# SwiGLU computed token-major with its norm gain in the activations, one token tile ahead at the mixer boundary, conformer taps in their own buffers

## The chip, the cores and the metric

One core of one Trainium2 chip runs the whole program. The metric is the device time of one execution in microseconds (us). Three executions of the kernel before are on record, and their median counts. Five engines work from queues of their own: TensorE (PE: matmuls and transposes), VectorE (DVE), ScalarE (ACT), GpSimd (POOL), and SyncE (SP), which issues nearly all transfers here.

## What is computed

One layer of a mixer and feed-forward block on 256 tokens, width 2048, feed-forward width 5632, all in float32:

```python
h = rms_norm(x, mix_pre_g)
proj = h @ w_in                       # hyena input, conformer a and b, two gates
hy_in, cf_a, cf_b = proj[..., :s1], proj[..., s1:s2], proj[..., s2:s3]
gate_a, gate_b = proj[..., s3:s4], proj[..., s4:]
...                                   # y_a: hyena long convolutions of hy_in
u = cf_a * sigmoid(cf_b)
u = depthwise_conv(u, cf_dw_w, cf_dw_b)          # the taps
y_b = silu(layer_norm(u, cf_ln_g, cf_ln_b))
merged = sigmoid(gate_a) * (y_a @ hy_proj) + sigmoid(gate_b) * (y_b @ cf_proj)
x = x + rms_norm(merged @ w_out, mix_post_g)
h = rms_norm(x, ffn_pre_g)
gu = h @ ffn_w_gu
gate, up = gu[..., :FFN_HIDDEN], gu[..., FFN_HIDDEN:]
x = x + rms_norm((silu(gate) * up) @ ffn_w_down, ffn_post_g)
```

## The kernel before

**Split products.** Each large matrix product is made of three rounded ones. An operand is split into a rounded part `hi` and the rest `lo`, and hi by hi, lo by hi and hi by lo are added up in PSUM. The activations are split once. The weights come as groups of 512 KB (2 x 128 rows by 512 columns): SP loads a group into one of four `raw` buffers (L288), ACT rounds it to `hi` (L301), DVE subtracts to get `lo` (L302); `hi` and `lo` have three buffers each, or come as `spare` ones from a pool of 35 slots called `big`. PE's matmuls are recorded on one line, L87.

**Stages.** In order: the input products with the hyena filters and convolutions; the gate chunks (weight `w_as`, 8 chunks of 512 columns each), beside which conformer and layer norm run; the two projections `hy_proj` and `cf_proj`; `w_out`; SwiGLU (`w_gu`, 11 gate chunks and 11 up chunks of 512 columns in turn); `w_down`. PSUM has four buffers called `main` and four called `aux`.

**Two forms of a chunk.** `chunk_as` is token-major: the split activations of 128 tokens are the stationary operand and 512 columns of weight move, so a chunk takes 96 matmuls 512 wide (8 groups, 2 halves, 2 token tiles, 3 products), in two PSUM buffers. `chunk_hl`, which SwiGLU uses, is feature-major: 128 columns of weight are stationary, and both token tiles and both parts of the activations move at once, 512 wide, for hi; for lo, 256 tokens move. That is 64 matmuls 512 wide and 64 matmuls 256 wide, in four buffers. There the norm's gain is multiplied into the weight in the split (ACT L306, DVE L307, two instructions each for a group), and 1/rms of each token is laid out along the free dimension by `per_token` (two matmuls at L450) and multiplied in twice on DVE (L1119, L1121).

**Order.** Each engine takes its instructions in the order of its queue. A scheduler of the framework sets that order from the program's order, priorities and dependences; `keep_in_program_order` and `in_order` (with the names L201 and L217 in the trace) pin some of it. The small steps of hyena, conformer, layer norm and norms are Python generators. `pump(budget)` runs a few of their steps after each weight group, so where their instructions stand depends on how many yields they make.

**The places the change touches.** `conformer` (L830) takes a `raw` buffer and a `hi` buffer of the weight rings for its taps: five small loads by SP (L835, L837), a cast on ACT (L839), a subtraction on DVE (L840). `layer_norm` transposes its result on PE (16 transposes, L890) and then, for four pairs of 128 features, runs two sigmoids on ACT (L897), two scalings on DVE (L898), a product on DVE (L900), a cast on ACT (L904) and a subtraction on DVE (L905). A gate chunk's PSUM buffers are emptied by ACT with a sigmoid (L811). At the mixer boundary, `turn` transposes the new residual stream for SwiGLU (PE L1012) and splits it (ACT and DVE, L201). `turn(0, ...)` handles token tile 0 while `w_out` ends. `turn_second` handles token tile 1, two feature tiles at a time, between the matmuls of SwiGLU's first chunk; it is preceded by `residual` (DVE L1003), and `keep_warm` puts 10 and 5 matmuls there whose result nobody reads.

Of the kernel before, what the change touches and what calls it, by code (L numbers as in the profile page):

```python
# [53 lines left out]
def block_kernel(ctx: ExitStack, tc: tile.TileContext, a: dict, out: bass.AP):  # L54
# [226 lines left out]
    def split_group(src, spare=False, gain=None, on=direct):  # L281

# [7 lines left out]
        return split_raw(raw, spare, gain, on)  # L290

    def split_raw(raw, spare=False, gain=None, on=direct, parts=False):
# [6 lines left out]
        if gain is None:  # L299
            for k in range(2) if parts else (slice(0, 2),):  # L300
                S.copy(hi[:, k], raw[:, k])  # L301
                V.tensor_tensor(out=lo[:, k], in0=raw[:, k], in1=hi[:, k], op=ALU.subtract)  # L302
        else:
# [87 lines left out]
    def product_as(w, nkt, act, budget, late, done):  # L391


        ps = [[aux() for _ in range(4)], [
            psm.tile([P, 512], F32, tag="main", name=nm("main")) for _ in range(4)]]
        groups = [(kt, hf) for kt in range(nkt) for hf in range(2)]
# [10 lines left out]
        held = []  # L407
        for i, (kt, hf) in enumerate(groups):
            ahead = i >= len(groups) - late
# [420 lines left out]
    def conformer(hf):  # L830
        cs = slice(hf * 512, (hf + 1) * 512)
        raw = wp.tile([P, 2, 512], F32, tag="raw", name=nm("raw"), bufs=4)
# [5 lines left out]
        wt = wp.tile([P, 2, 512], F32R, tag="hi", name=nm("hi"))  # L838
# [114 lines left out]
    drain(list(evac))  # L953
    evac.clear()
# [51 lines left out]
    def turn(t, kps):  # L1006

        ps = aux().rearrange("p (k q t) -> p k q t", k=2, t=P)
# [253 lines left out]
```

## Time and profile before

| what | value |
|---|---|
| three executions | 1409.57 to 1412.51 us, median 1412.0 |
| profiled execution | 1413.79 us, of it 1412.0 us in the profile's span |
| PE busy | 1392.8 us (99%) |
| DVE busy | 950.2 us (67%) |
| ACT busy | 740.2 us (52%) |
| SwiGLU, 715 to 1162 us | 20 chunks of 22.35 us each |

The profile follows the chain of work that ended last back from the last instruction. Where PE fills that chain, the time is the sum of PE's instructions plus the gaps between them; another engine's work counts only where PE waits for it. In the timeline, an instruction's own duration runs longer than the distance between two starts, since matmuls overlap: sums here use the distance between starts. A figure in square brackets behind a row is idle time of that engine just before it, with what ended it.

### The profile page before, as it was taken

How to read it: one execution, taken by the hardware profiler on the slowest of the kernel's cores; microseconds unless marked ns; L12 is line 12 of the kernel's file. 1: busy time of each engine (PE TensorE's matmuls, PEld its weight loads, DVE VectorE, ACT ScalarE, POOL GpSimd, SP SyncE). 2: the span in 40 equal slices, each digit the busy share in tenths (PEclk: the TensorE clock that was granted, in tenths of full speed). 3: DMA queues.
4: the chain of work that ended last, by engine and by line, in shares of the span. 5: the costliest groups of instructions: out<-in, count | busy, mean ns of one | idle time of the engine just before them, and what ended most of it. 6: DMA issues, size and time to landing. Idle time of an engine off the chain costs nothing.

```text
span 1412.0 us, 18734 instructions
## 1 busy us (share of the span) xinstructions
PE 1392.8 (99%) x7070; PEld 1183.2 (84%) x7070; DVE 950.2 (67%) x1378; ACT 740.2 (52%) x1093; POOL 11.0 (1%) x23
## 2 busy tenths in 40 slices
PE   9999999999899999999999999999999999999997
PEld 8788888888778888887888888888888888888885
DVE  5997978888878466547776767666666765444445
ACT  6665655455555444345665555555565654333343
POOL 0010000000000000000000000000000000000000
PEclk9999999999999999999999999999999999999999
DMA  9776554454455665765556666666666666666553
GB/s 331 216 211 179 171 188 147 148 152 133 153 173 167 196 189 179 273 197 171 163 186 190 181 195 189 193 184 191 189 185 193 185 190 222 194 193 193 193 188 128
DMA packets 76554, 264.70 MB, mean 187 GB/s; under 512 B 8689, under 2 KB 10002, under 8 KB 76464
## 3 DMA queue, kind: packets, MB, share of 16 engines
q1 hardware_dynamic: 75520, 261.74, 59.9%
q0 software_dynamic: 944, 1.77, 0.4%
q8 instruction: 55, 0.90, 0.2%
q14 instruction: 35, 0.29, 0.1%
HBM read 261.38 MB, written 2.10 MB: 187 GB/s over the span
## 4 chain that ended last, share of the span: by engine, by line
PE 93%; DMA 3%; DVE 2%; ACT 1%; issue 0%; DVEq 0%; SPq 0%; ACTq 0%
PE main L87 61%; PE aux L87 31%; DMA raw<-in_w_down_dram 1%; DMA raw<-in_w_out_dram 1%; DVE lo L302 1%; ACT big L301 0%; DVE big L302 0%; DMA raw<-in_w_gu_dram 0%; PE aux L1012 0%; DMA big<-in_xT_dram 0%; PE aux L934 0%; PE aux L620 0%; PE aux L704 0%; ACT hi L301 0%; PE aux L577 0%
## 5 line engine op out<-in xcount | busy, mean ns | idle before, releaser
L302 DVE TENSOR_TENSOR lo<-raw,hi 128x1024 fp32r<-128x1024 f32 x276 | 336.7, 1222 | 222.9 <-ACT hi L301 203.8
L301 ACT CAST hi<-raw 128x1024 fp32r<-128x1024 f32 x276 | 290.5, 1054 | 372.4 <-PE main L87 312.2
L87 PE MATMUL main<-hi,big 128*128 128x512 f32 x1440 | 369.8, 390 | 1.7 <-ACT hi L301 1.7
L307 DVE SCALAR_TENSOR_TENSOR lo<-raw,pv,hi 128x512 fp32r<-128x512 f32 x342 | 243.0, 747 | 153.0 <-ACT hi L306 150.6
L306 ACT ACTIVATE hi<-raw,pv 128x512 fp32r<-128x512 f32 x342 | 228.5, 716 | 188.3 <-PE aux L87 86.6
L87 PEld LDWEIGHTS main<-hi,big 128*128 128x128 f32 x1440 | 269.4, 188 | 57.9 <-ACT hi L301 2.2
L87 PE MATMUL main<-big,hi 128*128 128x512 f32 (+1 forms) x1152 | 278.9, 384 | 2.6 <-DVE t L734 1.2
L87 PEld LDWEIGHTS main<-big,hi 128*128 128x128 f32 x1152 | 201.5, 192 | 37.2 <-ACT hi L217 2.2
L87 PE MATMUL main<-lo,big 128*128 128x512 f32 x720 | 203.5, 390 | 2.0 <-DVE lo L302 2.0
L87 PE MATMUL aux<-big,hi 128*128 128x512 f32 x704 | 176.5, 392 | 0.0
L87 PEld LDWEIGHTS main<-lo,big 128*128 128x128 f32 x720 | 134.8, 188 | 30.7 <-DVE lo L302 2.6
L87 PEld LDWEIGHTS main<-big,lo 128*128 128x128 f32 x1088 | 149.1, 191 | 10.7
L87 PE MATMUL main<-big,lo 128*128 128x256 f32 x1088 | 152.9, 283 | 0.0
L87 PEld LDWEIGHTS aux<-big,hi 128*128 128x128 f32 x704 | 126.5, 189 | 22.6
L87 PE MATMUL aux<-hi,big 128*128 128x512 f32 x416 | 112.4, 389 | 0.0
L87 PEld LDWEIGHTS aux<-big,lo 128*128 128x128 f32 x704 | 96.2, 190 | 7.0
L87 PE MATMUL aux<-big,lo 128*128 128x256 f32 x704 | 98.3, 282 | 0.0
L87 PEld LDWEIGHTS aux<-hi,big 128*128 128x128 f32 x416 | 78.0, 188 | 16.2
L87 PE MATMUL aux<-big,big 128*128 128x512 f32 x288 | 78.3, 394 | 1.1 <-ACT big L301 0.8
L87 PE MATMUL aux<-lo,big 128*128 128x512 f32 x208 | 64.8, 389 | 0.0
L87 PEld LDWEIGHTS aux<-big,big 128*128 128x128 f32 x288 | 53.1, 188 | 13.8 <-ACT big L301 2.0
L87 PEld LDWEIGHTS aux<-lo,big 128*128 128x128 f32 x208 | 39.1, 188 | 8.1
(223 smaller groups left out, 804.9 us busy)
## 6 DMA issues: line engine op xcount, KB each, us to landing
raw<-in_w_gu_dram SPq DMA_DIRECT2D x176, 512.0 KB
raw<-in_w_as_dram SPq DMA_DIRECT2D x96, 512.0 KB
raw<-in_w_down_dram SPq DMA_DIRECT2D x88, 512.0 KB
raw<-in_w_in_dram SPq DMA_DIRECT2D x44, 512.0 KB
raw<-in_w_out_dram SPq DMA_DIRECT2D x32, 512.0 KB
raw<-in_hy_proj_dram SPq DMA_DIRECT2D x16, 512.0 KB
raw<-in_cf_proj_dram SPq DMA_DIRECT2D x16, 512.0 KB
raw<-in_w_in_dram SPq DMA_DIRECT2D x8, 256.0 KB
```

Of the source, the lines that this page charges most:

```text
L87: return nc.tensor.matmul(o, lhsT, rhs, start=start, stop=stop, skip_group_check=True)
L301: S.copy(hi[:, k], raw[:, k])
L302: V.tensor_tensor(out=lo[:, k], in0=raw[:, k], in1=hi[:, k], op=ALU.subtract)
L306: S.activation(hi[:, k], raw[:, k], AF.Identity, scale=g)
L307: V.scalar_tensor_tensor(out=lo[:, k], in0=raw[:, k], scalar=g, in1=hi[:, k], op0=ALU.mult, op1=ALU.subtract)
```

## The change

- **Taps.** The conformer's taps and their split get buffers from the slots of `big`, and the generator yields three times between the loads and the cast.
- **SwiGLU token-major.** `chunk_hl`, `joined` and the uses of `per_token` go. SwiGLU's chunks are `chunk_as`. The gain is applied where the activations are split: `turn` makes 128 x 128 instructions, one for each feature tile with its gain, in place of one for two feature tiles. 1/rms is a scale for each partition, in the Silu (L1103) and in the product on DVE (`glu_by`, L816). The product of both is token-major and is turned back for `w_down` by 8 PE transposes for each pair of chunks (L1113), then split (L1115, L1116).
- **First chunk.** `first_gate` runs token tile 0 of groups 0 to 2 ahead of tile 1, puts `turn_second` between, drops `keep_warm`, and splits from group 3 on one group ahead, with the split's instructions pinned behind `turn`'s on ACT and DVE.
- **`product_as`** (`w_out`, `w_down`) takes the first half of the columns for four row tiles before the second half, asks for its PSUM buffers in two steps, and drains waiting evacuations at the second step, where it had been done ahead of the stage.

```diff
-    def split_group(src, spare=False, gain=None, on=direct):
+    def split_group(src, spare=False, on=direct):
...
-            for k in range(2):
-                g = pv[:, gain + k:gain + k + 1]
-                S.activation(hi[:, k], raw[:, k], AF.Identity, scale=g)
-                V.scalar_tensor_tensor(
-                    out=lo[:, k], in0=raw[:, k], scalar=g, in1=hi[:, k],
-                    op0=ALU.mult, op1=ALU.subtract)
...
     def product_as(w, nkt, act, budget, late, done):
-        ps = [[aux() for _ in range(4)], [
-            psm.tile([P, 512], F32, tag="main", name=nm("main")) for _ in range(4)]]
-        groups = [(kt, hf) for kt in range(nkt) for hf in range(2)]
+        ps = [[], []]
+        first = 4
+        groups = [(kt, hf) for hf in range(2) for kt in range(first)]
+        groups += [(kt, hf) for kt in range(first, nkt) for hf in range(2)]
...
     def conformer(hf):
         cs = slice(hf * 512, (hf + 1) * 512)
-        raw = wp.tile([P, 2, 512], F32, tag="raw", name=nm("raw"), bufs=4)
+        raw = slot([P, 2, 512])
...
-        wt = wp.tile([P, 2, 512], F32R, tag="hi", name=nm("hi"))
+        wt = slot([P, 2, 512], F32R)
+        for _ in range(3):
+            yield None
         nc.scalar.copy(wt[:96], raw[:96])
...
     def turn(t, kps):
...
-        for i, kp in enumerate(kps):
-            turned.append(in_order(nc.scalar).copy(h2T[kp][:, :, 0, t * P:(t + 1) * P], ps[:, i]))
-        for i, kp in enumerate(kps):
-            d = h2T[kp][:, :, :, t * P:(t + 1) * P]
-            in_order(nc.vector).tensor_tensor(
-                out=d[:, :, 1, :], in0=ps[:, i], in1=d[:, :, 0, :], op=ALU.subtract)
+        parts = [(i, kp, q, pv[:, G_FFN + 2 * kp + q:G_FFN + 2 * kp + q + 1])
+                 for i, kp in enumerate(kps) for q in range(2)]
+        for i, kp, q, g in parts:
+            turned.append(S.activation(
+                h2T[kp][:, q, 0, tokens], ps[:, i, q], AF.Identity, scale=g))
+        for i, kp, q, g in parts:
+            V.scalar_tensor_tensor(
+                out=h2T[kp][:, q, 1, tokens], in0=ps[:, i, q], scalar=g,
+                in1=h2T[kp][:, q, 0, tokens], op0=ALU.mult, op1=ALU.subtract)
...
-            keep_warm(10, *warm)
         turn(1, (kp,))
         if kp == 0:
-            keep_warm(5, *warm)
             last()
...
-        per_token(rB, rstd2, psm.tile([P, 512], F32, tag="main", name=nm("main")))
...
-    def chunk_hl(w, col, gain, pool, tag, budget, turn=None):
...
+    def first_gate(w, budget):
+        ps = [psm.tile([P, 512], F32, tag="main", name=nm("main")) for _ in range(2)]
         on = (in_order(nc.scalar), in_order(nc.vector))
+        groups = KT // 2
+        parts = [split_group(w[g]) for g in range(3)]
+        def mms(g, t, ks=(0, 1)):
+            hi, lo = parts[g]
+            for k in ks:
+                av = h2T[g][:, k, :, t * P:(t + 1) * P]
+                for s, m in ((0, hi), (1, hi), (0, lo)):
+                    tc.keep_in_program_order(mm(
+                        ps[t], av[:, s], m[:, k, :], (g, k, s) == (0, 0, 0) and m is hi,
+                        (g, k) == (groups - 1, 1) and m is lo))
+        mms(0, 0)
+        mms(1, 0)
+        mms(2, 0, (0,))
+        turn_second(0)
+        mms(2, 0, (1,))
+        turn_second(1)
+        mms(0, 1)
+        for g in range(2, groups):
+            turn_second(g)
+            if g + 1 < groups:
+                parts.append(split_group(w[g + 1], g < 5, on))
+            mms(g - 1, 1)
+            if g + 1 < groups:
+                mms(g + 1, 0)
             pump(budget)
+        mms(groups - 1, 1)
         return ps
...
     def silu(ps, sg):
...
-            nc.vector.tensor_tensor(out=s, in0=s, in1=rB2, op=ALU.mult)
-            nc.scalar.activation(s, s, AF.Silu)
-            nc.vector.tensor_tensor(out=s, in0=s, in1=rB2, op=ALU.mult)
...
+        for t in range(2):
+            nc.scalar.activation(sg[:, t], ps[t], AF.Silu, scale=rstd2[:, t:t + 1])
+        yield 0.1
+    def glu(ps, sg, dst):
+        yield from glu_by(ps, sg, (rstd2[:, 0:1], rstd2[:, 1:2]))
         for i in range(2):
+            tr = aux().rearrange("p (c t) -> p c t", t=T)
+            for c in range(2):
+                for t in range(2):
+                    f = (2 * i + c) * P
+                    nc.tensor.transpose(tr[:, c, t * P:(t + 1) * P], sg[:, t, f:f + P], ident)
             d = dst[i]
-            nc.scalar.copy(d[:, :, 0, :], v)
-            nc.vector.tensor_tensor(out=d[:, :, 1, :], in0=v, in1=d[:, :, 0, :], op=ALU.subtract)
+            nc.scalar.copy(d[:, :, 0, :], tr)
+            nc.vector.tensor_tensor(out=d[:, :, 1, :], in0=tr, in1=d[:, :, 0, :], op=ALU.subtract)
...
-            chunk_hl(a["w_gu"], n * 512, G_FFN, psm, "main", 1.1,
-                     turn_second if n == 0 else None), sg))
+        after_chunk(silu(first_gate(w_gu[0], 1.2) if n == 0 else chunk_as(w_gu[n], h2T, 1.2), sg))
         before_chunk()
-        ps = chunk_hl(a["w_gu"], FFN + n * 512, G_FFN, psa, "aux", 1.1)
+        ps = chunk_as(w_gu[FFN // 512 + n], h2T, 1.2)
```

**Where instructions stand: the second load of the taps.** ACT's queue. `hi<-raw` at L301 (L299 now) is a weight group's cast; the cast of the taps is L839 (L841 now). Before:

```order
L301 CAST hi_3415<-raw_3413 128x1024
L301 CAST hi_3439<-raw_3437 128x1024
L680 COPY t_652_3290<-aux_3276 128x512
L839 CAST hi_3464<-raw_3457 96x1024
L301 CAST hi_3469<-raw_3467 128x1024
L711 ACTIVATE t_662_3337<-aux_3332,il_135 128x128
```

After:

```order
L662 CAST big_3431<-t_717_3551 128x512
L299 CAST hi_3908<-raw_3906 128x1024
L680 COPY t_733_3650<-aux_3635 128x512
L299 CAST hi_3926<-raw_3924 128x1024
L811 ACTIVATE big_3439<-main_3440,rstdx_124 128x512
L811 ACTIVATE big_3439<-main_3441,rstdx_124 128x512
L841 CAST big_3393<-big_3386 96x1024
L299 CAST hi_3965<-raw_3963 128x1024
L299 CAST hi_4004<-raw_4002 128x1024
```

On SP's queue the taps' loads stood directly ahead of the load of `raw_3467`, whose cast follows theirs on ACT. Now ten weight groups (`raw_3701` to `raw_3963`) are loaded between the taps' loads and the taps' cast.

**Layer norm, on ACT.** L897 (L899 now) is its sigmoid, L904 (L906) its cast, L811 the sigmoid that empties a gate chunk's PSUM. Before:

```order
L897 ACTIVATE t_827_4061<-aux_4056,pv 128x256
L301 CAST hi_4237<-raw_4235 128x1024
L897 ACTIVATE t_835_4095<-aux_4090,pv 128x256
L904 CAST big_4069<-t_829_4067 128x2x256
L301 CAST hi_4255<-raw_4253 128x1024
L897 ACTIVATE t_835_4095<-aux_4090,pv 128x256
L301 CAST hi_4273<-raw_4271 128x1024
L897 ACTIVATE t_843_4129<-aux_4124,pv 128x256
L904 CAST big_4103<-t_837_4101 128x2x256
L811 ACTIVATE big_3883<-main_3884,rstdx_124 128x512
L811 ACTIVATE big_3883<-main_3885,rstdx_124 128x512
L301 CAST hi_4294<-raw_4292 128x1024
```

After:

```order
L299 CAST hi_4332<-raw_4330 128x1024
L899 ACTIVATE t_822_4045<-aux_4040,pv 128x256 x2
L899 ACTIVATE t_830_4079<-aux_4074,pv 128x256
L906 CAST big_4053<-t_824_4051 128x2x256
L899 ACTIVATE t_830_4079<-aux_4074,pv 128x256
L899 ACTIVATE t_838_4113<-aux_4108,pv 128x256
L906 CAST big_4087<-t_832_4085 128x2x256
L899 ACTIVATE t_838_4113<-aux_4108,pv 128x256
L899 ACTIVATE t_849_4152<-aux_4147,pv 128x256
L906 CAST big_4121<-t_840_4119 128x2x256
L811 ACTIVATE big_3880<-main_3881,rstdx_124 128x512
L811 ACTIVATE big_3880<-main_3882,rstdx_124 128x512
```

Before, a weight cast stood between each two steps of layer norm, and L811 empties `main_3884` behind three of its four pairs. Now no weight cast stands between; the L811 for `main_3881` has the same place behind three pairs.

**Layer norm, on PE.** The last of its 16 transposes (L890, L892 now) and what follows. Before:

```order
L890 MATMUL aux_4124<-ident,big_3654 128x128
L890 MATMUL aux_4124<-ident,big_3655 128x128
L890 MATMUL aux_4124<-ident,big_3654 128x128
L890 MATMUL aux_4124<-ident,big_3655 128x128
L87 MATMUL main_4139<-hi_4142,big_115 128x512
L87 MATMUL main_4138<-lo_4143,big_115 128x512
L87 MATMUL main_4139<-lo_4143,big_115 128x512
L87 MATMUL main_4138<-lo_4143,big_115 128x512
L87 MATMUL main_4139<-lo_4143,big_115 128x512
L87 MATMUL main_4138<-hi_4165,big_116 128x512 x2
```

After:

```order
L892 MATMUL aux_4147<-ident,big_3652 128x128
L892 MATMUL aux_4147<-ident,big_3653 128x128
L892 MATMUL aux_4147<-ident,big_3652 128x128
L892 MATMUL aux_4147<-ident,big_3653 128x128
L87 MATMUL main_4125<-lo_4274,big_122 128x512
L87 MATMUL main_4126<-lo_4274,big_122 128x512
L87 MATMUL main_4125<-lo_4274,big_122 128x512
L87 MATMUL main_4126<-lo_4274,big_122 128x512
L87 MATMUL main_4290<-hi_4294,big_115 128x512 x4
```

Before, the transposes stood after the first 7 of the 96 matmuls of the chunk in `main_4138` and `main_4139`, so 89 followed. Now they stand ahead of the last 4 matmuls of the chunk in `main_4125` and `main_4126`; then comes the next chunk in `main_4290`, which takes over the buffer of `main_3881`.

**First chunk of SwiGLU, on PE.** L1012 (L1014 now) is a transpose of `turn_second`. Before, one group:

```order
L1012 MATMUL aux_5941<-ident,big_5122 128x128 x2
L87 MATMUL main_5823<-big_5132,hi_5845 128x512
L87 MATMUL main_5824<-big_5132,hi_5845 128x512
L87 MATMUL main_5825<-big_5132,hi_5845 128x512
L87 MATMUL main_5826<-big_5132,hi_5845 128x512
L87 MATMUL main_5823<-big_5132,lo_5846 128x256
L87 MATMUL main_5824<-big_5132,lo_5846 128x256
L87 MATMUL main_5825<-big_5132,lo_5846 128x256
L87 MATMUL main_5826<-big_5132,lo_5846 128x256
```

After, one group:

```order
L1014 MATMUL aux_5953<-ident,big_5105 128x128 x2
L87 MATMUL main_5839<-big_5911,big_5115 128x512 x2
L87 MATMUL main_5839<-big_5912,big_5115 128x512
L87 MATMUL main_5839<-big_5911,big_5115 128x512 x2
L87 MATMUL main_5839<-big_5912,big_5115 128x512
L87 MATMUL main_5838<-big_5963,big_5117 128x512 x2
L87 MATMUL main_5838<-big_5964,big_5117 128x512
L87 MATMUL main_5838<-big_5963,big_5117 128x512 x2
L87 MATMUL main_5838<-big_5964,big_5117 128x512
L1014 MATMUL aux_5979<-ident,big_5105 128x128 x2
```

Between two pairs of transposes there were 8 matmuls 512 wide and 8 matmuls 256 wide of groups split three ahead. Now there are 12 matmuls 512 wide: 6 of tile 1 with the group before (`big_5911`) and 6 of tile 0 with the group just split (`big_5963`).

## Rows read from the trace of the kernel before

**Rows 1.** The page: shares of the chain that ended last, by engine.

```profile
PE 93%; DMA 3%; DVE 2%; ACT 1%; issue 0%; DVEq 0%; SPq 0%; ACTq 0%
```

**Rows 2.** The chain in order of time: start, us, engine and line.

```profile
440.81 71.20 PE main L87 x314
...
1139.88 22.35 PE aux L87 x128
```

**Rows 3.** Busy time by window, PE first: SwiGLU, and the start of w_down.

```profile
715.00:1162.00 447.00, 447.00 (x2563) 393.31 (x2562) 299.39 (x482) 260.06 (x442) 0.00 (x0) 1.00 0.63 189
1162.00:1190.00 28.00, 28.00 (x126) 23.18 (x126) 15.89 (x18) 13.03 (x17) 0.00 (x0) 1.00 0.68 227
```

**Rows 4.** Timeline of PE at the second load of the taps.

```profile
358.28 2.11 PE L87 MATMUL main<-hi,big 128*128 128x512 f32 x8 [1.71 <-ACT hi L301]
...
365.68 1.21 PE L87 MATMUL main<-lo,big 128*128 128x512 f32 x4 [2.04 <-DVE lo L302]
```

**Rows 5.** Timeline of ACT, then of SP, at the second load of the taps.

```profile
356.24 1.05 ACT L839 CAST hi<-raw 96x1024 fp32r<-96x1024 f32 x1 [4.46 <-PE aux L704]
...
345.49 0.95 SPq L835 DMA_DIRECT2D raw<-in_cf_dw_w_dram  x3
```

**Rows 6.** Timeline of PE, matmuls 512 and 256 wide in one chunk.

```profile
696.90 1.12 PE L87 MATMUL aux<-big,lo 128*128 128x256 f32 x8
697.86 2.00 PE L87 MATMUL aux<-big,hi 128*128 128x512 f32 x8
```

**Rows 7.** The chain at the 16 transposes of layer norm.

```profile
439.06 1.75 PE aux L890 x16
```

**Rows 8.** Timeline of ACT in layer norm.

```profile
439.76 0.57 ACT L897 ACTIVATE t<-aux,pv 128x256 f32<-128x256 f32 x1 [2.10 <-PE aux L890]
440.94 0.56 ACT L897 ACTIVATE t<-aux,pv 128x256 f32<-128x256 f32 x1 [0.61 <-DVE t L898]
...
442.84 0.62 ACT L904 CAST big<-t 128x512 fp32r<-128x512 f32 x1
...
453.94 1.27 ACT L811 ACTIVATE big<-main,rstdx 128x512 f32<-128x512 f32 x2
```

**Rows 9.** Timeline of DVE in layer norm.

```profile
441.54 0.54 DVE L898 TENSOR_SCALAR t<-aux,pv 128x256 f32<-128x256 f32 x1 [0.64 <-ACT t L897]
442.12 0.69 DVE L900 TENSOR_TENSOR t<-t,t 128x512 f32<-128x512 f32 x1
442.73 1.22 DVE L302 TENSOR_TENSOR lo<-raw,hi 128x1024 fp32r<-128x1024 f32 x1
```

**Rows 10.** The chain at the mixer boundary and the first chunk.

```profile
664.28 2.28 PE aux L87 x10
...
667.22 1.15 PE aux L87 x5
...
672.43 0.22 PE aux L1012 x2
...
715.01 0.22 PE main L450 x2
```

**Rows 11.** Timeline of DVE, then ACT (two rows), at the boundary and at L711.

```profile
666.22 0.48 DVE L1003 SCALAR_TENSOR_TENSOR big<-big,por,big 128x256 f32<-128x256 f32 x1
...
672.68 0.37 ACT L201 CAST big<-aux 128x256 fp32r<-128x256 f32 x1 [0.74 <-PE aux L1012]
...
358.14 0.36 ACT L711 ACTIVATE t<-aux,il 128x128 f32<-128x128 f32 x1
```

**Rows 12.** Busy time by window of 1 us, granted clock third from the end.

```profile
46.00:47.00 1.00, 0.00 (x0) 0.00 (x0) 1.00 (x4) 0.03 (x1) 0.00 (x0) 1.00 1.12 252
47.00:48.00 1.00, 0.92 (x3) 0.81 (x4) 1.00 (x4) 1.00 (x3) 0.00 (x0) 0.78 0.92 145
...
50.00:51.00 1.00, 1.00 (x4) 0.79 (x3) 1.00 (x4) 0.00 (x0) 0.00 (x0) 0.52 0.91 307
...
350.00:360.00 10.00, 8.29 (x42) 6.67 (x40) 4.72 (x6) 4.35 (x11) 0.00 (x0) 1.00 0.48 139
```

More of the change, by code (lines that the diff above doesn't have):

```diff
@@ L289, in split_group, with split_raw @@
         latest[:] = [raw]
-        return split_raw(raw, spare, gain, on)
-    def split_raw(raw, spare=False, gain=None, on=direct, parts=False):
+        return split_raw(raw, spare, on)
+    def split_raw(raw, spare=False, on=direct, parts=False):
         if spare:
@@ L298, in split_raw @@
         S, V = on
[L299 to L303, printed above, removed]
-            for k in range(2):
-                g = pv[:, gain + k:gain + k + 1]
-                S.activation(hi[:, k], raw[:, k], AF.Identity, scale=g)
-                V.scalar_tensor_tensor(
-                    out=lo[:, k], in0=raw[:, k], scalar=g, in1=hi[:, k],
-                    op0=ALU.mult, op1=ALU.subtract)
+        for k in range(2) if parts else (slice(0, 2),):
+            S.copy(hi[:, k], raw[:, k])
+            V.tensor_tensor(out=lo[:, k], in0=raw[:, k], in1=hi[:, k], op=ALU.subtract)
         return hi, lo
@@ L407, in product_as @@
         held = []
+        before_chunk()
         for i, (kt, hf) in enumerate(groups):
+            if kt == 0:
+                if hf:
+                    drain(list(evac))
+                    evac.clear()
+                ps[0] += [aux() for _ in range(2)]
+                ps[1] += [psm.tile([P, 512], F32, tag="main", name=nm("main")) for _ in range(2)]
             ahead = i >= len(groups) - late
@@ L1049, in block_kernel @@
     post_norm(a["w_out"], KT, mT, "mix_post_g", "po", 1.3, 8, finish_mixer, turn_first)
-    rB = const.tile([P, 1, T], F32, name="rB")
     def h_norm():
@@ L1058, in h_norm @@
             rms_rstd(rstd2[:, t:t + 1], ss2[:, t, :], f"pf{t}")
-        yield None
-        per_token(rB, rstd2, psm.tile([P, 512], F32, tag="main", name=nm("main")))
         done.add("h_norm")
-    rB2 = rB.broadcast_to([P, 2, T])
-    def chunk_hl(w, col, gain, pool, tag, budget, turn=None):
-        ps = [pool.tile([P, 2, T], F32, tag=tag, name=nm(tag)) for _ in range(4)]
-        def split(g):
-            ahead.append(split_group(
-                w[col // 512, g], gain=gain + 2 * g, on=on if turn and g > 2 else direct))
-        ahead = deque()
-        on = (in_order(nc.scalar), in_order(nc.vector))
-        if turn:
-            for g in range(3):
-                split(g)
-            turn(0)
-        for g in range(KT // 2):
-            if not turn:
-                split(g)
-            hi, lo = ahead.popleft()
-            for k in range(2):
-                for c in range(4):
-                    m = mm(ps[c], hi[:, k, c * P:(c + 1) * P], h2T[g][:, k],
-                           g == 0 and k == 0, False)
-                    if turn:
-                        tc.keep_in_program_order(m)
-                if turn and k == 0 and g + 1 < KT // 2:
-                    turn(g + 1)
-            for k in range(2):
-                for c in range(4):
-                    m = mm(ps[c][:, 1, :], lo[:, k, c * P:(c + 1) * P], h2T[g][:, k, 0, :],
-                           False, g == KT // 2 - 1 and k == 1)
-                    if turn:
-                        tc.keep_in_program_order(m)
-            if turn and g + 3 < KT // 2:
-                split(g + 3)
@@ L1124, in glu @@
-    def glu(ps, sg, dst):
-        up = slot([P, 4, T])
-        yield from joined(ps, up)
-        for i in range(2):
-            v = up[:, 2 * i:2 * i + 2, :]
+        for t in range(2):
[3 more added lines that the diff above has]
+        yield from glu_by(ps, sg, (rstd2[:, 0:1], rstd2[:, 1:2]))
+        for i in range(2):
+            tr = aux().rearrange("p (c t) -> p c t", t=T)
[3 more added lines that the diff above has]
+                    nc.tensor.transpose(tr[:, c, t * P:(t + 1) * P], sg[:, t, f:f + P], ident)
@@ L1129, in glu @@
             d = dst[i]
[L1130 to L1133 removed]
+            nc.scalar.copy(d[:, :, 0, :], tr)
+            nc.vector.tensor_tensor(out=d[:, :, 1, :], in0=tr, in1=d[:, :, 0, :], op=ALU.subtract)
+            yield 0.7
+    w_gu = a["w_gu"]
     for n in range(FFN // 512):
```

21 lines of the change are left out of this document (3 added, 18 removed).

## The prediction

> **What bounds the kernel now.** I read the chain's shares first: PE fills 93% of it [rows 1]. The chain in order of time then shows long pieces of PE with nothing between, 314 matmuls in 71.20 us and twenty chunks of SwiGLU at 22.35 us each [rows 2]; by windows PE is busy without a gap over the whole of SwiGLU and the start of `w_down` [rows 3]. So two things change the time: how many us of instructions PE has, and where PE waits. The work that the change takes off DVE and ACT inside SwiGLU (two products with 1/rms, one gain in each split) is worth nothing by itself, since PE never waits for them there. Then I looked at the three places where the change alters what PE waits for: the taps, layer norm, and the first chunk.
>
> **Taps: -3.75.** PE waits 1.71 us for a cast and 2.04 us for the subtraction a little later [rows 4]. The releaser named is a weight's cast, but that cast stood behind the taps' cast (L839), which ACT began at 356.24 after 4.46 us idle; the taps had been issued by SP at 345.49 [rows 5], so they took 10.7 us to be of use. Now ten weight groups lie between their loads and their cast. A group is 12 matmuls in a gate chunk, 71.20 / 314 = 0.2268 us each [rows 2], so 2.72 us; ten, less the four that the `raw` buffers let SP run ahead, are 16 us, more than 10.7. The wait goes: -3.75. If the loads were later still, the sum would lack it.
>
> **Layer norm: +8.4, and +1.7 for the clock.** The three extra yields and the later loads move the conformer about a chunk back, and layer norm with it. Its 16 transposes stood at the start of a gate chunk, with 89 matmuls (20.2 us) behind them for PE; now 4 matmuls stand between them and a chunk whose first PSUM buffer is emptied by an L811 that stands on ACT behind three of layer norm's four pairs. I count from the first transpose, y. PE: 1.75 [rows 7] and 4 x 0.2268, done at y + 2.66. ACT: the weight cast ahead of layer norm needs the buffer that PE frees at y, so it ends about 1.35 later (1.05 for such a cast by L839 [rows 5], 0.3 to its start), and the first sigmoid begins at y + 1.35. DVE's scaling follows 0.60 later (440.94 to 441.54 [rows 8, 9]); then 0.46, a weight's subtraction that now stands between (1.22, 1.14 apart), and 0.58 to the product (441.54 to 442.12 [rows 9]): y + 4.13. The cast of the pair starts 0.72 behind the product (442.12 to 442.84 [rows 8, 9]): y + 4.85. A further pair costs DVE product, scaling, subtraction and scaling at 0.61, 0.69 (waiting for the cast), 0.63 and 0.58, so 2.5 us; two make the third cast start at y + 9.95. It takes 0.50, and the L811 0.63 for one tile (1.27 for two [rows 8]): y + 11.1. PE waits 11.1 - 2.66 = **8.4**. Before, the same L811 began at 453.94 [rows 8], some 7 us ahead of the chunk that needed its buffer (440.8 + 89 x 0.2268 = 461.0), which is why no wait shows. The range: nothing if the emptying came first; 10 if a step of ACT or DVE here takes as long as in the trace of before, where a pair lasted 5 us between weight casts.
>
> After an idle stretch PE starts slower. PE stood idle through 46 to 47 us, and the granted clock was then 0.78 in the next us and 0.52 in the fourth, half in between; the four lose 0.22 + 0.50 + 0.50 + 0.48 = 1.7 us. With 8.3 of 10 us busy the clock stayed at full level [rows 12]. An idle stretch of 8 us is like the first: **+1.7**, with 0 and 3.5 as ends.
>
> **First chunk and boundary: +2.45, and +1.7 for the clock.** Before, from the end of `w_out` at 664.28 to the end of the second chunk at 715.23 are 50.95 us [rows 10]. Of these, `keep_warm` is 3.43 (2.28 + 1.15) and `per_token` 0.44 (two pieces of 0.22) [rows 10]. Now the two chunks are 192 matmuls of 0.2268, 43.55 us, and the 16 transposes cost 1.75 as before [rows 7]: 45.3 without waits, 5.65 less. `keep_warm` was no loss while PE had to wait anyway, so I count the waits that come:
> - Ahead of `turn_second(0)`: 15 matmuls (3.4 us) cover to 667.7. The first `residual` began on DVE at 666.22 [rows 11]; DVE now has 16 instructions of 128 columns in place of 8 of 256 ahead of it (0.25 apart on ACT by L711 [rows 11], a little more on DVE), about 1.5 later. It ends at 668.2 to 668.7: 0.9.
> - Ahead of `turn_second(1)`: 3 matmuls cover 0.7 of the split, `last()` and the next `residual`, 2.2 in all: 1.5.
> - Groups 3 to 6. After two transposes (0.22) ACT splits them, beginning 0.41 after the transposes began (672.43 against about 672.7 [rows 10, 11]), two at 0.25, then the group's cast, 1.05: `hi` is ready at 1.97. DVE's subtraction, 1.22 [rows 9], makes `lo` ready at 3.2. PE has 6 matmuls to fill, to 1.58; it waits 0.4 for `hi`, does two, waits 0.8 for `lo`, does four. A group takes 4.14 instead of 2.94: 4 x 1.2 = 4.8. Before, the weights were split further ahead and PE had no such wait: from 672.43 on only the transposes' 0.22 lies between long pieces.
> - The last group and the start of the second chunk, two casts and two subtractions against 14 matmuls: 0.9.
>
> Together 8.1, so -5.65 + 8.1 = **+2.45**. Ends: -3 (only the first waits come), +5. The first two waits lie close together, 2.4 us idle of 3.3, nearer to the stretch at 46 us than to the one at 350 us [rows 12]: **+1.7** more, 0 to 3.5.
>
> **SwiGLU's other twenty chunks: -2.0.** A chunk took 22.35 [rows 2]; 96 matmuls at 0.2268 are 21.77: -0.58, times 20, -11.6. It is the narrow matmul that is dear: eight 256 wide take 0.96 (696.90 to 697.86 [rows 6]), so 0.12 each, more than half of 0.2268. The turning back adds 8 transposes for each of 11 pairs, 88 x 1.75 / 16 [rows 7] = +9.6. Their tile is multiplied on DVE two groups ahead of them, and DVE and ACT are busy 299 and 260 of 447 us there [rows 3], with less to do now, so I cost waits at nothing; one wait of 0.5 us in each pair would be +5.5.
>
> The Trainium skill, "TensorE: Matmul & The Clock Gate", section "Back-to-back issue gap", gives an isolated gap of N/2.4 GHz + 2.5 ns. By that rule 64 wide and 64 narrow matmuls take an estimated 20.80 us and 96 wide ones 20.72, so the twenty chunks would gain 1.6 us instead of 11.6, and the sum would be 10 us higher. The rows disagree: 0.2268 against its 0.2158 and 0.12 against its 0.109, a fixed part some four to eight times as large. The rows decide.
>
> **`product_as` and the drains: 0.** `w_out`'s first groups ask for fewer PSUM buffers at first, which can only start earlier; the drains moved into it cost ACT and DVE what they did. Into `w_down` PE has no gap to win [rows 3]. From -1 to +2.
>
> **Sum.** -3.75 + 8.4 + 1.7 + 2.45 + 1.7 - 2.0 = +8.5. The profiled execution's span of 1412.0 becomes 1420.5, its whole time 1413.8 becomes 1422.3; the median before, 1412.0, lies as far below that execution as the span does, so I forecast 1420.5 for the median.
>
> **Rivals.**
> - *Layer norm does not hold PE up.* If the L811 is done when PE comes, 8.4 and 1.7 go: 1410.4, no change. For it: it was so before. Against: the order of ACT's queue and 4 matmuls as the only cover.
> - *Faster: ACT and DVE are ahead of PE in both places.* If a group's cast runs before the transposes' splits, as groups 0 to 2 are cast early, the first chunk has no waits either: -3.75 - 5.65 - 2.0 = -11.4, 1400.6. It decides whether ACT reaches the cast of group 3 before PE's transposes of feature tile 2. Against: these splits are pinned ahead of it.
> - *More idle, longer slow clock.* The small gaps of 1.2 us in each 4.1 us keep the clock at half through the first chunk: 16 us of it at half adds up to 6: 1426.5.
> - *The taps' wait is not removed, only moved:* +3.75, 1424.3. For it: SP's queue stays in order and their loads still come behind ten groups. Against: 16 us of lead.
>
> **How the numbers follow.** Forecast 0.60; layer norm free 0.17; faster 0.09; slow clock 0.08; taps 0.06. Forecast's own ends, from the clock terms and a pair's cadence, are 1416 to 1425. The range 1408 to 1427 leaves out the faster case and the tails. A measurement of this kernel tells 0.2%, 2.8 us, from no change. Faster: 0.09 and a third of the layer-norm case, 0.14. Same: the rest of it, 0.13. Slower: 0.73.
>
> **What would show it.** Two gaps gone at the taps; one PE gap of 8 us, released by ACT at L811, right after the transposes at L892, with a clock below 1.00 behind it; gaps of 0.4 and 0.8 us in turn at the first chunk, released by the cast and the subtraction; later chunks of 21.8 us, with 0.87 for transposes in every second one. I am wrong if PE's gap at layer norm is below 3 us, or if a late chunk is not 21.8.

## The result, and the profile after

The kernel after takes 1420.0 us (median of four executions, 1417.69 to 1423.05) against 1411.29 us for the kernel before (1409.57 to 1412.51). The ratio is 1.0064, 95% interval 1.0041 to 1.0087: slower by 5.8 to 12.3 us. The forecast was 1420.5.

PE has less to do and waits more. The page's line of busy time, engine by engine (busy us, share of the span, instructions):

```profile
PE 1387.0 (98%) x6435; PEld 1151.6 (81%) x6435; DVE 868.9 (61%) x1084; ACT 670.3 (47%) x844; POOL 9.3 (1%) x23
```

DVE lost 81 us of work and ACT 70, and the time rose all the same. What PE waited for in the kernel after (engine and line, what it waited for: us in total, times, longest):

```profile
PE main L87 <- ACT big L811: 9.4, 2, 8.9
PE aux L1014 <- DVE big L1003: 2.2, 2, 1.7
PE main L87 <- DVE big L201: 1.6, 3, 0.5
...
PE main L87 <- ACT big L201: 0.8, 3, 0.3
...
PE main L87 <- DVE lo L201: 0.5, 1, 0.5
PE main L87 <- ACT hi L201: 0.5, 2, 0.3
```

None of these waits was there before (one of 0.41 us for the residual stood elsewhere, at token tile 0's transposes); the two waits of 1.71 and 2.04 us at the taps [rows 4] are gone. Of the first line, 8.85 us are layer norm's place and 0.59 a gate chunk before it, at 402.06; the others are the first chunk of SwiGLU.

**Layer norm.** Timeline of PE around its 16 transposes, then of ACT and one row of DVE beside it (start, us, engine, line, operation, count; idle time ahead in brackets, with what ended it):

```profile
451.88 1.91 PE L892 MATMUL aux<-ident,big 128*128 128x128 f32 x16
453.55 1.17 PE L87 MATMUL main<-lo,big 128*128 128x512 f32 x4
463.57 2.07 PE L87 MATMUL main<-hi,big 128*128 128x512 f32 x4 [8.85 <-ACT big L811]
```

```profile
453.03 0.56 ACT L899 ACTIVATE t<-aux,pv 128x256 f32<-128x256 f32 x1
...
457.19 0.62 ACT L906 CAST big<-t 128x512 fp32r<-128x512 f32 x1 [1.97 <-DVE t L902]
...
459.75 0.62 ACT L906 CAST big<-t 128x512 fp32r<-128x512 f32 x1 [1.02 <-DVE t L902]
...
462.31 0.62 ACT L906 CAST big<-t 128x512 fp32r<-128x512 f32 x1 [1.02 <-DVE t L902]
462.83 1.26 ACT L811 ACTIVATE big<-main,rstdx 128x512 f32<-128x512 f32 x2
```

```profile
454.75 1.23 DVE L300 TENSOR_TENSOR lo<-raw,hi 128x1024 fp32r<-128x1024 f32 x1 [0.58 <-PE main L87]
```

Three casts at steps of 2.56 us, each waiting for DVE's product, then L811, then PE. Before, a weight cast stood between such steps, PE had 89 matmuls in hand, and nobody waited [rows 8].

Then the granted clock, the third number from the end, in windows of 1 us at the end of that gap and behind it, and one window at the first chunk:

```profile
463.00:464.00 1.00, 0.43 (x1) 0.43 (x2) 0.65 (x1) 1.00 (x3) 0.00 (x0) 0.50 0.00 0
464.00:465.00 1.00, 1.00 (x3) 0.73 (x3) 0.41 (x1) 0.55 (x2) 0.00 (x0) 0.50 0.06 16
467.00:468.00 1.00, 1.00 (x4) 0.76 (x4) 0.23 (x1) 0.67 (x2) 0.00 (x0) 0.66 0.00 0
468.00:469.00 1.00, 1.00 (x6) 0.81 (x5) 0.00 (x0) 0.00 (x0) 0.00 (x0) 1.00 0.00 0
...
673.00:674.00 1.00, 0.00 (x0) 0.00 (x0) 1.00 (x4) 0.00 (x0) 0.00 (x0) 1.00 0.00 0
```

From 463.57 to 468 PE worked at half clock, the lower of its two levels (1.2 in place of 2.4 GHz): 0.43 x 0.5 + 3 x 0.5 + 0.34 = 2.05 us lost. From 673 to 674 us PE is idle, and the clock stays at 1.00.

**First chunk.** Timeline of PE, then DVE:

```profile
671.73 0.44 PE L1014 MATMUL aux<-ident,big 128*128 128x128 f32 x2 [0.54 <-DVE big L1003]
...
674.52 0.44 PE L1014 MATMUL aux<-ident,big 128*128 128x128 f32 x2 [1.65 <-DVE big L1003]
...
676.20 0.38 PE L1014 MATMUL aux<-ident,big 128*128 128x128 f32 x2
...
678.23 0.73 PE L87 MATMUL main<-big,big 128*128 128x512 f32 x2 [0.27 <-ACT big L201]
679.49 1.18 PE L87 MATMUL main<-big,big 128*128 128x512 f32 x4 [0.53 <-DVE big L201]
680.51 0.38 PE L1014 MATMUL aux<-ident,big 128*128 128x128 f32 x2
```

```profile
677.81 0.47 DVE L1003 SCALAR_TENSOR_TENSOR big<-big,por,big 128x256 f32<-128x256 f32 x1
678.21 1.23 DVE L201 TENSOR_TENSOR big<-raw,big 128x1024 fp32r<-128x1024 f32 x1
```

A group takes 4.31 us from transposes to transposes (676.20 to 680.51) where its work is 12 x 0.2268 + 0.22 = 2.94. Bracketed idle times understate this, as matmuls overlap: the distance of starts counts.

**Later chunks.** The chain in order of time:

```profile
727.85 0.87 PE aux L1113 x8
728.73 43.55 PE main L87 x192
772.27 0.87 PE aux L1113 x8
```

Two chunks at 21.78 us and 0.87 for turning back: 44.42 for a pair, where it was 44.70 [rows 2].

**The sum in the two profiled executions**, stage by stage. The second chunk's end of the kernel after is 727.85 less the 24 matmuls of the third chunk that precede the first L1113, 722.4; `w_out` ends at 667.8: PE's next piece begins at 667.63 in the timeline, and the chain's figures lie 0.16 later, as 664.28 against 664.12 before.

| stage | before | after | change | forecast |
|---|---|---|---|---|
| start to the last of the hyena's transposes (L620) | 306.89 | 304.34 | -2.55 | 0 |
| from there to the end of `w_out` | 357.4 | 363.45 | +6.05 | +6.35 |
| end of `w_out` to the end of the second chunk | 50.95 | 54.6 | +3.65 | +2.45, clock +1.7 |
| twenty chunks, with all transposes | 447.0 | 445.05 | -1.95 | -2.0 |
| `w_down` and the end, without the last transposes | 249.8 | 248.4 | -1.35 | 0 |
| span | 1412.0 | 1415.9 | +3.9 | +8.5 |

The profiled pair differs by less than the medians, 3.9 against 8.7: of the two kernels' executions it was the longest of before and the shortest of after. The first line is chance: the clock fell in the first 60 us in the one, which cost 1.7 us [rows 12], and not in the other, and the kernel before without `keep_warm`, whose clock held there, came to this point at 304.94. The last line and a part of the second are short waits for weights and for the residual that the profiled execution of before had, and this one had not. Timeline of PE, before:

```profile
641.54 8.91 PE L87 MATMUL aux<-big,big 128*128 128x512 f32 x38 [0.43 <-ACT big L301]
658.11 1.62 PE L1012 MATMUL aux<-ident,big 128*128 128x128 f32 x8 [0.41 <-DVE big L1003]
...
1387.95 0.97 PE L87 MATMUL aux<-big,big 128*128 128x512 f32 x3 [0.38 <-ACT big L301]
1389.21 3.01 PE L87 MATMUL aux<-big,big 128*128 128x512 f32 x12 [0.29 <-DVE big L302]
```

By the distance of starts these waits cost about 1.3 us in each of the two stages. Other kernels here have such waits at other places (0.74 at 653 us without the yields, 1.34 at 1374 us with both edits), so I take them for chance too.

### The profile page after: what moved, and what is told of

Read it like the earlier page. It is cut to its first block, busy times and chain, and to the rows that moved or that the text cites. A ratio compares the mean times of both kernels' runs of the same rounds, so it can differ in the third digit from the quotient of the medians.

```text
span 1415.9 us, 16893 instructions
## 1 busy us (share of the span) xinstructions
PE 1387.0 (98%) x6435; PEld 1151.6 (81%) x6435; DVE 868.9 (61%) x1084; ACT 670.3 (47%) x844; POOL 9.3 (1%) x23
## 4 chain that ended last, share of the span: by engine, by line
PE 50%; DVE 0%; ACT 0%; DVEq 0%; issue 0%
PE main L87 41%; PE aux L87 8%; PE aux L1113 1%; DVE big L1135 0%; ACT hi L299 0%; ACT hi L201 0%; DVEq L1239 0%; DVE big L201 0%; ACT pd1y L201 0%; DVE pd1t L201 0%; ACT t L272 0%; PE aux L1014 0%; DVE pd1y L201 0%; DVE pdr L201 0%
## 5 line engine op out<-in xcount | busy, mean ns | idle before, releaser
L300 DVE TENSOR_TENSOR lo<-raw,hi 128x1024 fp32r<-128x1024 f32 x447 | 546.3, 1224 | 450.5 <-ACT hi L299 427.4
L299 ACT CAST hi<-raw 128x1024 fp32r<-128x1024 f32 x447 | 471.4, 1056 | 645.4 <-PE main L87 589.3
L87 PE MATMUL main<-hi,big 128*128 128x512 f32 x2824 | 719.5, 391 | 10.2 <-ACT big L811 9.4
L87 PEld LDWEIGHTS main<-hi,big 128*128 128x128 f32 x2824 | 528.8, 188 | 121.2 <-ACT big L811 10.5
L87 PE MATMUL main<-lo,big 128*128 128x512 f32 x1412 | 393.4, 390 | 0.5 <-DVE lo L201 0.5
L87 PEld LDWEIGHTS main<-lo,big 128*128 128x128 f32 x1412 | 265.0, 188 | 56.5 <-DVE lo L201 1.0
L87 PE MATMUL main<-big,hi 128*128 128x512 f32 (+1 forms) x448 | 98.2, 363 | 2.6 <-DVE t L734 1.2
L87 PEld LDWEIGHTS main<-big,hi 128*128 128x128 f32 x448 | 73.8, 191 | 14.9 <-ACT hi L217 2.1
L87 PEld LDWEIGHTS main<-big,lo 128*128 128x128 f32 x384 | 52.2, 190 | 3.4
L87 PE MATMUL main<-big,lo 128*128 128x256 f32 x384 | 54.0, 282 | 0.0
L299 ACT CAST big<-raw 128x1024 fp32r<-128x1024 f32 x16 | 16.8, 1052 | 18.0 <-DMA raw<-in_w_out_dram 9.0
L816 DVE SCALAR_TENSOR_TENSOR big<-main,rstd,big 128x512 f32<-128x512 f32 x22 | 15.5, 747 | 11.9 <-PE main L87 11.9
```

What stands on the lines that cost most here:

```text
L87: return nc.tensor.matmul(o, lhsT, rhs, start=start, stop=stop, skip_group_check=True)
L816: nc.vector.scalar_tensor_tensor(out=d[:, t], in0=ps[t], scalar=scale[t], in1=d[:, t], op0=ALU.mult, op1=ALU.mult)
```

## Experiments

My theory: layer norm's place costs some 11 us (a gap at L811 and the slow clock behind it), and the empty yields put it there; the first chunk's waits cost as much as its matmuls save, and the split's place behind `turn_second` is their cause. Rivals: the first chunk alone, or the taps' buffers, or the stages of `product_as`. Ratios below are against the kernel before, run on the same chip.

**No empty yields.**

```diff
         wt = slot([P, 2, 512], F32R)
-        for _ in range(3):
+        for _ in range(0):
             yield None
         nc.scalar.copy(wt[:96], raw[:96])
```

> The kernel after with one thing undone: the three empty yields between the loads of the conformer's taps and their cast are gone, the taps keep their own buffers. In the order of instructions layer norm's 16 transposes then stand near the start of a gate chunk again, as in the kernel before, with most of the chunk's matmuls behind them. My theory (PE's gap of 8.9 us and the slow clock behind it come from where the yields put layer norm): the gap is under 0.5 us, the clock stays at full level there, and the time falls by 8.9 + 2.05 = 11 us against the kernel after, to about 1409 us. Rival (the gap comes from the taps' own buffers or from later loads, not from the yields): the gap stays above 6 us, time within 3 us of 1420. Open beside it: whether the two PE waits at the second load of the taps (1.71 + 2.04 us) come back; if the yields were what removed them, 3.75 us of the 11 return, 1413.

Measured: 1410.49 us, ratio 0.9997 (0.9984 to 1.0010), 9.5 us less than the kernel after. The gap shrank to 1.8 us, not to nothing: timeline of PE of this kernel, then of ACT and of SP at the second load of the taps:

```profile
456.41 1.19 PE L87 MATMUL main<-hi,big 128*128 128x512 f32 x4 [1.83 <-ACT big L811]
```

```profile
351.28 1.05 ACT L841 CAST big<-big 96x1024 fp32r<-96x1024 f32 x1 [4.79 <-DMA big<-in_cf_dw_b_dram]
```

```profile
339.31 0.96 SPq L835 DMA_DIRECT2D big<-in_cf_dw_w_dram  x3
```

Two things follow. The yields put layer norm where it hurt. And the taps' waits on PE did not come back without them, though ACT still stood 4.79 us for the loads: SP issued them at 339.31 in place of 345.49 [rows 5], and ACT's cast began at 351.28 in place of 356.24. Of both differences 1.8 us are this execution's earlier arrival at L620 (305.10 against 306.89). The rest fits the buffers: before, SP stood idle from 341.25 to 345.49 ahead of these loads, which needed a `raw` buffer to come free, and here they follow the load before them at once. The buffers removed those waits; the yields were not needed for it. What else this kernel changes comes later, from `w_out` on.

**The conformer's part alone**, put into the kernel before:

```diff
-        raw = wp.tile([P, 2, 512], F32, tag="raw", name=nm("raw"), bufs=4)
+        raw = slot([P, 2, 512])
...
-        wt = wp.tile([P, 2, 512], F32R, tag="hi", name=nm("hi"))
+        wt = slot([P, 2, 512], F32R)
+        for _ in range(3):
+            yield None
```

> The kernel before with the conformer's part of the change alone (own buffers for the taps and the three yields); SwiGLU, boundary and stages of w_out and w_down as before. My theory: two waits of 3.75 us gone, a gap of 8.9 us at layer norm and 2.05 us of slow clock come, and 0.6 us of wait at an earlier chunk: +7.8 us against the kernel before, about 1419 us. Rival (what makes the kernel after slower is the first chunk and the boundary, and the conformer's part comes out even): within 2 us of the kernel before, 1411.

Measured: 1417.4 us, ratio 1.0054 (1.0038 to 1.0069): 5.4 to 9.7 us slower, the expected 7.8 within. PE's first wait in its list:

```profile
PE main L87 <- ACT big L811: 9.4, 2, 8.8
```

So this small part brings 6.3 us of loss by the medians, where the whole change brings 8.7, with nothing else altered, and the rival that the conformer's part comes out even is wrong.

**Four yields in place of three.**

```diff
-        for _ in range(3):
+        for _ in range(4):
             yield None
```

> The kernel after with four empty yields in place of three. In the order of instructions layer norm's transposes stand at the same place, ahead of the last 4 matmuls of a gate chunk, but the sigmoid that empties the buffer which the next chunk takes (L811) stands on ACT behind two of layer norm's four pairs, not three. My theory (PE waits for exactly that L811, and each pair ahead of it costs one step of 2.55 us): the gap is 8.85 - 2.55 = 6.3 us, released by ACT at L811. Rival (PE's gap is the whole of layer norm on ACT and DVE, or the weight casts held up behind it): still 8 to 9 us, or longer.

Measured, one execution of 1417.4 us; PE's wait list, then ACT's timeline:

```profile
PE main L87 <- ACT big L811: 6.3, 1, 6.3
```

```profile
456.85 0.62 ACT L906 CAST big<-t 128x512 fp32r<-128x512 f32 x1 [1.97 <-DVE t L902]
...
459.41 0.62 ACT L906 CAST big<-t 128x512 fp32r<-128x512 f32 x1 [1.02 <-DVE t L902]
459.93 1.26 ACT L811 ACTIVATE big<-main,rstdx 128x512 f32<-128x512 f32 x2
```

One pair fewer ahead of L811, 2.55 us less, as expected to a tenth. The gap is this queue and not layer norm as a whole. The gap does not go with the number of yields: none gave 1.8 us, three 8.9, four 6.3.

**The split ahead of `turn_second`.**

```diff
-            turn_second(g)
             if g + 1 < groups:
                 parts.append(split_group(w[g + 1], g < 5, on))
+            turn_second(g)
```

> The kernel after with one line moved: in the first chunk the next group of weights is split ahead of turn_second's instructions for the group, not behind them. My theory (each of the four groups' 1.4 us of lost time comes from the cast standing behind the transposes' splits on ACT): a group goes from 4.33 us to about 2.95 us, four of them give back 5.5 us, and the time is about 1414.5 us. Rival (DVE is the bound of this stretch: residual, split of the transposes and subtraction follow one another there): a group stays above 3.9 us, under 2 us are given back.

Measured: 1411.96 us, ratio 1.0012 (1.0003 to 1.0022), 8 us below the kernel after. PE's transposes in this kernel:

```profile
675.77 0.38 PE L1014 MATMUL aux<-ident,big 128*128 128x128 f32 x2
...
678.74 0.38 PE L1014 MATMUL aux<-ident,big 128*128 128x128 f32 x2
...
681.71 0.38 PE L1014 MATMUL aux<-ident,big 128*128 128x128 f32 x2
```

A group takes 2.97 us now. Four groups and a similar last step give back 6.4 us by the trace (the stretch from 676.20 to 699.33 of the kernel after is 23.1 us, here 16.7). That is all by which the two profiled executions differ (6.3); the medians differ by 8, and I did not find the rest. DVE, the rival's bound, does the same work in that time.

**The old `product_as`**, drains included, in the kernel after:

```diff
-        ps = [[], []]
-        first = 4
-        groups = [(kt, hf) for hf in range(2) for kt in range(first)]
-        groups += [(kt, hf) for kt in range(first, nkt) for hf in range(2)]
+        ps = [[aux() for _ in range(4)], [
+            psm.tile([P, 512], F32, tag="main", name=nm("main")) for _ in range(4)]]
+        groups = [(kt, hf) for kt in range(nkt) for hf in range(2)]
...
```

> The kernel after with the stages of w_out and w_down as in the kernel before (old order of their first groups, PSUM buffers asked for at once, evacuations drained ahead of the stage). My theory: this part of the change is worth nothing, within 1.5 us of the kernel after, about 1420 us. Rival (the stretch from the projections to the end of w_out hides a gain or a loss of this part): a difference of 3 us or more, seen between the end of the gate chunks and the end of w_out or in the gaps of w_down.

Measured: 1418.81 us, ratio 1.0061 (1.0043 to 1.0078) against the whole change's 1.0064. This part is worth nothing that can be told. The traces say the same: from the first transpose of `cf_proj`'s chunks to the first at the boundary both kernels take 144.97 us, and from the last turning back to PE's last matmul 234.1 here and 234.0 in the kernel after.

**No turning back.**

```diff
-            tr = aux().rearrange("p (c t) -> p c t", t=T)
-            for c in range(2):
-                for t in range(2):
-                    f = (2 * i + c) * P
-                    nc.tensor.transpose(tr[:, c, t * P:(t + 1) * P], sg[:, t, f:f + P], ident)
+            tr = sg[:, :, 2 * P * i:2 * P * (i + 1)]
```

> The kernel after without the 88 PE transposes that turn SwiGLU's hidden tiles back: their split reads the token-major tile directly, so the hidden activations stand in the wrong layout and w_down's result is a different one. My theory (the transposes cost PE their own time and no wait): 88 x 0.109 = 9.6 us less, SwiGLU's pairs of chunks at 43.55 us each without a piece of 0.87 between, no other change. Rival (they also cost waits, or are partly hidden): the distance between pairs falls by more or less than 0.87 us.

Measured in one execution, 1409.83 us; the chain shows SwiGLU as one piece:

```profile
701.95 457.90 PE main L87 x2020
```

In the kernel after, the same 2020 matmuls and ten of the eleven sets of transposes take 466.9 us (699.71 to 1166.60): 9.0 less without them, 8.7 of it by the rows. Transposes cost their own time, and nothing hides it.

**`keep_warm` taken out of the kernel before.**

```diff
             residual(1, og, rstd, 0)
-            keep_warm(10, *warm)
         turn(1, (kp,))
         if kp == 0:
-            keep_warm(5, *warm)
             last()
```

> The kernel before without keep_warm's 15 matmuls at the mixer boundary, whose result nobody reads. My prediction counted them as no loss while PE had to wait there anyway, and as what might keep the clock up. That theory: PE has two waits of about 1.5 to 3 us together in their place, the time stays within 1.5 us of the kernel before (1411), or is up to 1.7 us longer where the clock falls. Rival (they were work on PE's path): 3.4 us less, about 1407.6.

Measured: 1412.54 us, ratio 1.0013 (1.0004 to 1.0022), 0.6 to 3.1 us longer. PE waited in its place, 2.33 us and then 0.92 us, and the clock fell (windows of 1 us, the first at the taps, the others at the boundary):

```profile
366.00:367.00 1.00, 1.00 (x4) 0.81 (x3) 1.00 (x3) 1.00 (x3) 0.00 (x0) 0.50 0.82 336
...
666.00:667.00 1.00, 0.65 (x2) 0.24 (x2) 0.00 (x0) 0.32 (x1) 0.00 (x0) 0.50 0.00 0
...
671.00:672.00 1.00, 1.00 (x4) 0.81 (x4) 0.33 (x1) 0.19 (x1) 0.00 (x0) 0.50 0.00 0
672.00:673.00 1.00, 1.00 (x8) 1.00 (x8) 0.00 (x0) 1.00 (x2) 0.00 (x0) 0.77 0.00 0
```

So the matmuls that nobody reads earned their 3.4 us, and the change's first chunk did without them. The fall at the taps, at 365 us, has nothing to do with them: the waits there are those of the kernel before, whose clock stayed at 1.00 behind them.

**Both mended, and two steps further.** The first kernel has no yields and the split ahead. The second moves a piece of the residual ahead too. The third is the second with eight yields.

```diff
         if kp == 0:
             residual(1, og, rstd, 0)
+            residual(1, og, rstd, 1)
         turn(1, (kp,))
         if kp == 0:
             last()
-        for k in range(1, 3) if kp == 0 else range(kp + 2, min(kp + 3, 8)):
+        for k in range(2, 3) if kp == 0 else range(kp + 2, min(kp + 3, 8)):
             residual(1, og, rstd, k)
```

> The kernel after with the two edits at once: no empty yields at the taps, and the next group's split ahead of turn_second's instructions in the first chunk. My theory (the two losses are in different stretches and add up): 1420 - 9.5 - 8 = 1402.5 us, between 1401 and 1406; against the kernel before about 0.6% faster. Rival (PE gets to the next stage earlier and meets transfers or other engines there): 1408 us or more.

> The kernel e7_both_mended with one more edit: in turn_second's first call the second piece of the residual on DVE stands ahead of the transposes' split and of the last product of the norm, not behind them. My theory (PE's wait of 1.65 us ahead of the second pair of transposes is DVE's order): that wait falls below 0.4 us, and with it the slow clock that follows in some executions; 1 to 3 us faster than e7_both_mended. Rival (DVE has the same work in front of the matmuls that follow, so that the wait moves behind the next transposes): the waits of the stretch keep their sum, time as e7_both_mended within 1 us.

> The kernel e8_residual_ahead with eight empty yields at the taps in place of none. In the order of instructions the L811 that empties the buffer of the chunk after layer norm then stands on ACT ahead of all of layer norm, and weight casts stand between layer norm's steps again. My theory (the 1.8 us that PE still waits at that L811 come from its place behind layer norm's pairs): no gap at L811 above 0.3 us, and 1.8 to 3 us faster than e8_residual_ahead, about 1400.5. Rival (layer norm's work has to be waited for at some place): the gap moves to the next chunk's L811 or to the projections, and the time stays within 1 us of e8_residual_ahead, 1403.

Measured: 1404.67 us (ratio 0.9957, 0.9943 to 0.9970), 1402.88 us (0.9945, 0.9932 to 0.9958) and 1400.74 us (0.9932, 0.9918 to 0.9945). The first is 15.3 below the kernel after, 2 us short of the sum of the two edits but within the range expected. Of PE's waits, the first kernel's; then PE's timeline in the second, from `turn_second`'s first pair of transposes to its fourth:

```profile
PE aux L1014 <- DVE big L1003: 2.2, 2, 1.6
PE main L87 <- ACT big L811: 1.8, 1, 1.8
```

```profile
665.09 0.44 PE L1014 MATMUL aux<-ident,big 128*128 128x128 f32 x2 [0.55 <-DVE big L1003]
...
666.06 0.38 PE L1014 MATMUL aux<-ident,big 128*128 128x128 f32 x2
...
667.90 0.41 PE L1014 MATMUL aux<-ident,big 128*128 128x128 f32 x2
...
670.94 0.38 PE L1014 MATMUL aux<-ident,big 128*128 128x128 f32 x2
```

The wait of 1.65 us ahead of the second pair is gone, as expected, and did not move behind the next transposes: these four pairs span 5.85 us, where they spanned 7.43 in the first kernel (663.05 to 670.48). So the trace shows 1.6 us. The medians' step, 1.8 us, is inside what the two intervals can tell, and so is the step of 2.1 us to the third kernel, which ran on another chip. The wait of 1.8 us at L811 is still there in the second kernel. In the third the wait at L811 is gone; by windows, PE was busy through the whole of layer norm at full clock:

```profile
440.00:475.00 35.00, 35.00 (x165) 29.20 (x164) 27.06 (x41) 19.68 (x26) 0.00 (x0) 1.00 0.62 191
```

This version beats both kernels: 0.55 to 0.82% faster than the kernel before.

## Why the prediction was right

- *Taps, -3.75.* Right in size: no wait is left there (by the distance of starts the two waits had cost 4.4). Its reason was partly wrong. I put it down to ten groups of lead that the yields give; without yields the waits stay away too, by the buffers.
- *Layer norm, +8.4 and +1.7.* Measured 8.85 (9.0 by the distance of starts) and 2.05. The walk through the queues holds but for one step: first sigmoid 1.15 behind the first transpose (1.35 said), casts 2.56 apart (the sum took 2.55, though it says 2.5), L811 at 10.95 (10.5). The step is DVE's subtraction of a weight ahead of the first product. It began 1.12 behind the scaling (453.63 to 454.75), where I had counted 0.46, since it waited 0.58 for PE. A second wait at L811, 0.6 us at an earlier gate chunk, I did not see coming.
- *First chunk, +2.45 and +1.7 for the clock.* Measured +3.65 and no clock loss in the profiled execution. The waits were 9.1 in place of 8.1. The step that was mis-sized is the group: 4.32 us in place of 4.14. DVE does a piece of the residual (0.40) between the transposes' split and the weight's subtraction, which my count left out, but it cost next to nothing: ACT's cast ran until 678.18, and the subtraction began at 678.21. `lo` was ready 3.24 behind the transposes (3.2 said); PE went on at 3.29, and its four matmuls up to the next transposes took 1.02 in place of 0.91. Waits of 0.7 and 1.8 came at the two `turn_second` steps (0.9 and 1.5 said), and 1.1 at the last group (0.9). The clock term did not show there: 673 to 674 us is idle and the clock stays at 1.00. In the kernel without yields it came down behind the same wait of 1.65 us, to 0.61 and 0.50 in the windows that follow, and the next pair of transposes stood 3.05 us behind (666.37 to 669.42) in place of 1.68: 1.4 us. So this term comes in some executions and not in others, and should have been an end of the range, not a part of the sum.
- *Twenty chunks, -2.0.* Measured -1.95; the price of the transposes is confirmed by taking them out. The rows decided rightly: a chunk went from 22.35 to 21.78. By an estimate from the formula for an isolated gap in the Trainium skill, "TensorE: Matmul & The Clock Gate", section "Back-to-back issue gap", the two forms would have cost nearly the same; the trace after disagrees, with 0.57 us a chunk.
- *`product_as`, 0.* Confirmed.

The chances at the end of the prediction are a little off: 0.09 and a third of 0.17 are 0.15, and the rest of the 0.17 is 0.11. The sum of the terms agrees with the medians to a microsecond, closer than its parts deserve, and that closeness is luck. At layer norm the waits and the clock came to 11.9 us by the distance of starts, 0.9 of it at the earlier L811, where I had 10.1. The taps gave back 4.4 and not 3.75. At the first chunk the clock was counted too much, the waits there too little. The stage up to the end of `w_out` agrees (6.05 against 6.35) only because 1.3 us of short waits fell away there too. Read so, my terms come to some +9.2 in the profiled pair; the start of the program (-2.55) and the short waits (twice -1.3), which no term of mine contains, bring it down to +3.9.

## What to carry to other kernels

An empty yield in a background step of such a scheduler can change the order on other engines: look where the next stage's PSUM emptying stands on its engine's queue and how many matmuls PE has in hand at that point, since that is what decides whether a serial chain of small steps on two other engines is free or holds PE up (here for 9.0 of the 11.7 us from the first transpose to the matmul that waited). Where a group's weights are split one group ahead, put the cast ahead of the instructions that wait for this group's transposes, not behind them. An engine relieved of 70 or 80 us of work gave nothing here, and a wait that a few idle matmuls had covered is not to be uncovered without pricing the clock.

## What the runs showed of the hardware

After the same wait the clock fell in one execution and not in another. Seven profiled kernels have the wait of 1.65 us for the residual at the first chunk. The granted clock stayed at 1.00 behind it in five of them, the kernel after among these, and fell to 0.50 in two, those of "No empty yields" and of "Four yields". The wait of 1.8 us at L811 left it at 1.00 in "No empty yields" and in the first of the mended kernels, and it fell to 0.50 behind it, at 458 to 460 us, in the second. The waits at the taps left it at 1.00 in the kernel before, and in the kernel without `keep_warm` it fell to 0.50 behind them for 366 to 368 us. The first 60 us of the kernel before show it below 1.00 for four windows [rows 12], those of the kernel after do not. The idle stretch at layer norm, 6.3 us in one execution and 8.8 to 8.9 us in five, was followed by half clock in all six (2.05 us lost in the kernel after). In the kernel without `keep_warm` the clock was at half for six windows at the boundary, and a second wait, of 0.92 us, fell into them. The executions of one kernel lie up to 5.4 us apart here for the kernel after (four of them) and up to 9.0 us for the kernel without yields (ten). Such stretches are a part of that; the rest I did not trace.
